# Grouped-query score maxima taken from high parts alone, in pairs on 64 rows each, eight pairs a chunk

## The chip, the cores and the metric

One core of one Trainium2 chip runs the whole kernel. The metric is the device time of one execution in microseconds. The engines are TensorE (PE in the profile; its weight loads are PEld), VectorE (DVE), ScalarE (ACT), GpSimd (POOL) and SyncE (SP, which issues most transfers). Each takes its own queue in order.

## The reference, cut to what matters

An encoder block on 2048 tokens of width 1024, in float32. Two groups of heads run side by side: multi-head latent attention (MLA, 8 heads of 96 dimensions) and grouped-query attention (GQA, 8 query heads of 64 dimensions on 2 key/value heads). Both are softmax attention over all 2048 keys:

```
s = jnp.einsum('bkgqd,bskd->bkgqs', qblk.astype(jnp.float32), kf) * scale
p = jax.nn.softmax(s, axis=-1)
return jnp.einsum('bkgqs,bskd->bkgqd', p, vf)
```

Norms and an axial rotation on queries and keys come before, an output projection, a residual add and a dense SwiGLU network behind.

## The kernel before

Operands of matmuls are split into a high part that fits the fast float32r format and a low part that holds the rest; a product is then high x high + high x low + low x high.

Four stages follow each other: the input projections (to about 440 us), attention (440 to 1885 us), the output projection, and the dense network. The change lies in attention, and a little in the end of the first stage.

Attention goes by chunks of 512 queries: 4 chunks a head, the 8 GQA heads first (chunks 0 to 31), then the 8 MLA heads (32 to 63). Within a chunk it goes by 16 key tiles of 128 keys; `g` counts key tiles over all chunks. For each key tile:

- `score` (L732, L733): two matmuls into a bank `sc`, keys on the stationary side. For GQA `kk` holds the high part of the keys on 64 rows and the low part on the other 64, `qh` holds the high queries twice, so one matmul of 128 rows gives high x high + low x high; the second adds high keys (`k1`) x low queries, and on a 65th row the shift, minus the query's maximum.
- `expo` and `high` (L742, L752, ACT): the exponential, and its high part `ph`. `low` (L756, DVE): its low part `pl`. In 4 of a GQA chunk's 16 tiles the low part is made by POOL, and a matmul with `tail1` (L795) adds up the rows.
- `pv_high`, `pv_low` (L786, L796): products with the values into the banks `px` and `py`.

At a chunk's end come `out_copy`, `out_x`, `out_y` (ACT L802, DVE L806, L810), `out_mm` (L819, L820: eight small matmuls on PE into an `mx` bank) and `out_div` (four small DVE operations, L827 to L830).

The shift needs the maxima ahead of the scores. `max_mm` (L702) computes a block of 128 queries x 512 keys roughly, for GQA with `qh` against `kk`; `max_reduce` (L707, DVE) takes its row maxima into `cm`. A chunk has 16 such blocks, numbered `m`; after the last, L709 (DVE) joins them, `shift_mm` (L713, PE) transposes them, and `shift_row` (L717, ACT) puts them, through a DMA, into the operand's extra row. Blocks run 24 ahead of the scores; the first 24 (`EARLY`) stand in the first stage.

PSUM has eight banks: 4 for `sc`, 2 for `mx`, 1 each for `px` and `py`. A tile of `mx` takes the two banks in turn and waits until the reader of the tile before the last is done. `mx` serves the maximum blocks, L713's output, `out_mm`, and for a few tiles of the first stage done late (`late_mm`, one set of four transposes in each of eight chunks) their transposes.

The order of PE, ACT, DVE and POOL is written out by a table: each operation gets a time in units of one key tile (`at`), operations are sorted by it, and every engine runs its own in that order. `GQA` and `MLA` hold the offsets: `S` for the score, `C` and `B` for high and low, `M` for the block of the maximum, `R` for its reduction, `Sh` and `Sc` for the shift. An `at` never goes ahead of the last one of the same function.

Of the kernel before, what the change touches and what calls it, by code (L numbers as in the profile page):

```python
# [20 lines left out]
P = 128  # L21
S = 2048
NT = S // P
D = 1024
KD = D // P
QL, KVL, ROPE, NOPE, QK, VD = 384, 256, 32, 64, 96, 64
H = 8
HD = 64
# [8 lines left out]
CH = 512  # L37
LK = H * QK
NCH = S // CH

# [6 lines left out]
def hybrid_block_kernel(  # L47
# [7 lines left out]
    nc = tc.nc  # L55
# [7 lines left out]

    d_qh = dram.tile([H, QK, S], F32, name="d_qh")
    d_ql = dram.tile([H, QK, S], F32, name="d_ql")
    d_kh = dram.tile([H, QK, S], F32, name="d_kh")
    d_kl = dram.tile([H, QK, S], F32, name="d_kl")
    d_gqh = dram.tile([H, HD, S], F32, name="d_gqh")
    d_gql = dram.tile([H, HD, S], F32, name="d_gql")
    d_gkh = dram.tile([GKV, HD, S], F32, name="d_gkh")  # L70
    d_gkl = dram.tile([GKV, HD, S], F32, name="d_gkl")
# [19 lines left out]
    def pst(tag=None):  # L91

        uid[0] += 1
        if "a" in pools:
            return pools["a"].tile([P, CH], F32, tag="pa", name=f"pa_{uid[0]}")
        if tag is None:
            tag = TURN[turn[0] % len(TURN)]
            turn[0] += 1
        return pools["b"].tile([P, CH], F32, tag=tag, name=f"{tag}_{uid[0]}", bufs=BANKS[tag])
# [4 lines left out]
    def fetch(dst, src):  # L104
        nc.sync.dma_start(dst.bitcast(F32), src)
# [439 lines left out]
    for t in range(3, LAST):  # L545
# [31 lines left out]
    EXB, PHB, PLB = 3, 5, 6  # L577
    AHEAD = 24
    EARLY = 24
    LATE = 29.4  # L580
    HEADAT = 12

    GQA = dict(
        S=-1.6, E=-0.05, C=0.6, B=1.2, Cq=0.85, Bp=1.9, A=1.4, M=1.7, R=0.65, Sh=1.6, Sc=1.9, px=5.45,
        py=7.45, X=0.6, Y=0.75, Z=0.7, T=3.6, D=1.49,
        dx=[0.0, -0.5, -0.5, -0.5, -0.3, 0.0, -0.3, -0.6, -0.6, -0.35, -0.35, -0.35, -0.35, 0.4, 0.4, -0.1],
        dy=[0.6, 0.55, 0.35, 0.35, 0.35, 0.35, 0.35, 0.35, 0.35, 0.35, 0.1, 0.1, 0.1, 0.1, 0.1, 0.1],
# [2 lines left out]
        S=-1.75, E=-0.05, C=0.7, B=1.4, Cq=0.8, Bp=1.4, A=1.35, M=-4.1, R=0.5, Sh=1.6, Sc=1.2, px=5.9,  # L592
# [11 lines left out]
    def load_head(n):  # L604
        h = ORDER[n]
        hd = heads[n] = {"mla": h < H, "col": h * VD}
        todo = []
        if h < H:
            hd["kh"] = kh = op.tile([QK + 1, S], F32R, tag="op0", name=f"kh_{h}")
            hd["kl"] = kl = op.tile([QK, S], F32R, tag="op1", name=f"kl_{h}")  # L610
            todo += [(kh[0:QK, :], d_kh[h]), (kl, d_kl[h])]
            one = kh[QK:QK + 1, :]
            vi = h
        else:
            g = h - H
            vi = H + g // (H // GKV)
            one = None
            if vi in shared:
                hd["kk"], hd["k1"], hd["v"] = shared[vi]
            else:  # L620
                hd["kk"] = kk = op.tile([P, S], F32R, tag="op0", name=f"kk_{h}")
                hd["k1"] = k1 = op.tile([HD + 1, S], F32R, tag="op1", name=f"k1_{h}")
                e = vi - H
                todo += [(kk[0:HD, :], d_gkh[e]), (kk[HD:P, :], d_gkl[e]), (k1[0:HD, :], d_gkh[e])]
                one = k1[HD:HD + 1, :]
        if n == 0:
            cut = S - 2 * P
            for dst, src in todo:
                fetch(dst[:, 0:cut], src[:, 0:cut])
            late.extend((dst[:, cut:S], src[:, cut:S]) for dst, src in todo)  # L630
        else:
            for dst, src in todo:
                fetch(dst, src)
        if one is not None:
            fetch(one, d_one)
            hd["v"] = v = op.tile([P, NT, VW], F32R, tag="opv", name=f"v_{h}")
            if n == 0:
                cut = LAST - 2
                fetch(v[:, 0:cut], d_v[vi][:, 0:cut])
                late.append((v[:, cut:], d_v[vi][:, cut:]))  # L640
            else:
                fetch(v, d_v[vi])
            if h >= H:
                shared[vi] = hd["kk"], hd["k1"], v
# [24 lines left out]
    cms, pms, pcs, scs, exs, phs, pls = {}, {}, {}, {}, {}, {}, {}  # L669
    accs, pxs, pys, o65s, pts = {}, {}, {}, {}, {}  # L670

    def mla(u):
        return heads_mla[u // NCH]
# [3 lines left out]
    def pace(u):  # L677
        return MLA if mla(u) else GQA
# [5 lines left out]
    def block(m):  # L684

        u, r = divmod(m, NT)
        return (u, r % 4, r // 4) if u == 0 else (u, r // 4, r % 4)

    def max_mm(m):
        u, qt, kc = block(m)  # L690
        hd = heads[u // NCH]
        if m % NT == 0:
            cms[u] = (bs.tile([P, 4, 4], F32, tag="cm", name=f"cm_{u}"),
                      bs.tile([P, 4], F32, tag="cx", name=f"cx_{u}"))
        qh = qs[u, 0]
        qt_ = slice(qt * P, (qt + 1) * P)
        ks = slice(kc * CH, (kc + 1) * CH)
        pms[m] = pm = pst("mx")
        if hd["mla"]:
            nc.tensor.matmul(pm, qh[0:QK, qt_], hd["kh"][0:QK, ks], start=True, stop=True)  # L700
        else:
            nc.tensor.matmul(pm, qh[:, qt_], hd["kk"][:, ks], start=True, stop=True)  # L702

    def max_reduce(m):
        u, qt, kc = block(m)
        cm, cx = cms[u]
        nc.vector.tensor_reduce(out=cm[:, qt, kc:kc + 1], in_=pms.pop(m), axis=AX.X, op=ALU.max)  # L707
        if m % NT == NT - 1:
            nc.vector.tensor_reduce(out=cx, in_=cm, axis=AX.X, op=ALU.max)  # L709
# [143 lines left out]
        transpose_split(d["mh"], d["ml"], o_sb[t // 4][:, t % 4, :], KD)  # L853

    def max_block(m):
        max_mm(m)
        max_reduce(m)


# [12 lines left out]
    def late_part(t, nm, b0, which):  # L872
        hi, lo = (room["qk".index(nm)][0:QK].rearrange("p (s h c) -> p s h c", s=2, c=P)[:, i] for i in range(2))
        t4_parts(banks[t, nm, b0], nm, b0, hi, lo, which)
        if b0 > 0 and which == "l":
            t4_store(t, nm, hi, lo)

    load_head(0)
    for u in range(QHB - 1):
        load_q(u, 0)  # L880
# [10 lines left out]
    for m in range(4):  # L891
        max_block(m)
# [7 lines left out]
    for m in range(4, 8):  # L900
        max_block(m)
# [4 lines left out]
    for m in range(8, 12):  # L906
        max_block(m)
# [28 lines left out]
    def at(key, fn, *args):  # L936
        key = max(key, latest.get(fn, key))
        latest[fn] = key
        ops.append((key, len(ops), fn, args))
        return key  # L940

    for g in range(TOTAL):
        u, kt = divmod(g, NT)
        i, q = g // 2, pace(u)
# [12 lines left out]
        if kt == NT - 1:  # L957
            at(kx + q["X"], out_copy, u)
            k = at(kx + q["Y"], out_x, u)
            k = at(max(k + 0.01, ky + q["Z"]), out_y, u)  # L960
            k = at(k + q["T"], out_mm, u)
            at(k + q["D"], out_div, u)
    for m in range(EARLY, TOTAL):
        u = m // NT
        q = pace(u)
        k = m - AHEAD + q["M"]
        at(k, max_mm, m)
        k = at(k + q["R"], max_reduce, m)
        if m % NT == NT - 1:
            k = at(k + q["Sh"], shift_mm, u)  # L970
            at(k + q["Sc"], shift_row, u)
    for n in range(1, len(ORDER)):
        at((n - 1) * NCH * NT + HEADAT if n > 1 else -99, load_head, n)
# [5 lines left out]
    for n, t in enumerate((LAST - 1, LAST)):  # L979
        k = LATE + 4 * n * NT  # L980
        at(k - 11, late_load, t)
# [275 lines left out]
    with tc.tile_pool(name="dg", reuse_waits="tile", bufs=6) as dg:  # L1257
# [19 lines left out]
        for T in range(2):  # L1277
# [4 lines left out]
            u = dg.tile([P, 4, CH], F32, tag="u", name=f"u_{T}", bufs=1)  # L1282
# [94 lines left out]
```

## Time and profile before

| | before |
|---|---|
| median of 3 runs | 3373.79 us (3369.88 to 3375.1) |
| profiled execution | 3374.82 us, span 3373.0 us |
| PE / DVE / ACT / POOL busy | 99% / 80% / 58% / 49% of the span |
| one GQA chunk (792.20 to 813.30) | 21.10 us: DVE busy 19.79, ACT 18.40, POOL 18.01 |
| granted TensorE clock | 0.997 of full speed |

A row of the timeline is: start in us from the span's start, how long it took, engine, line, operation, what it writes and reads, shapes, count, and in brackets the idle time of the engine ahead of it with what ended it. A row of the groups (section 5 of the page) ends with busy us, mean ns of one, and idle us ahead. A row of the waits is: who waited, for whom, us in total, how often, the longest. Ends of matmuls are modelled, so two starts tell more than a matmul's length.

### The profile page before, as it was taken

Reading aid. Unit: us, or ns where it says so; the run is one execution under the profiler, and the core shown is the slowest. Engines: PE = TensorE matmul, PEld = TensorE weight load, DVE = VectorE, ACT = ScalarE, POOL = GpSimd, SP = SyncE. Lnnn points to the kernel's source line nnn. Section 1 sums busy time; section 2 is a strip of 40 time slices with the busy share of each in tenths; the row PEclk is TensorE's granted clock in tenths of the full one; section 3 lists DMA queues with packets and bytes.
Section 4 is the critical chain, followed back from the end, with each engine's and each line's share of the span. In section 5 each row is a group of like instructions: output and inputs, shape, how many; then the busy total and the mean of one; then the engine's idle time right before and its main releaser. Section 6 shows DMA issues by size and latency. Waiting matters only on the chain.

```text
span 3373.0 us, 47535 instructions
## 1 busy us (share of the span) xinstructions
PE 3342.7 (99%) x15722; PEld 2693.6 (80%) x15722; DVE 2699.0 (80%) x4844; ACT 1967.5 (58%) x3726; POOL 1659.5 (49%) x1152
## 2 busy tenths in 40 slices
PE   8999999999999999999999999999999999999999
PEld 7999967777777777777777788878878888888887
DVE  6777799999999899999999656777787767776574
ACT  5444478888888778787878634332343333344443
POOL 4445478888887777777777301332312222130020
PEclk9999999999999999999999999999999999999999
DMA  5665621201000211111110456545464344486664
GB/s 175 148 146 135 152 75 48 60 20 51 20 20 14 70 48 50 51 46 32 34 51 19 129 179 235 181 146 159 156 198 143 125 146 145 146 273 229 219 199 164
DMA packets 330192, 390.96 MB, mean 116 GB/s; under 512 B 20719, under 2 KB 219980, under 8 KB 325264
## 3 DMA queue, kind: packets, MB, share of 16 engines
q1 hardware_dynamic: 329122, 387.72, 37.9%
q8 instruction: 124, 2.03, 0.2%
q14 instruction: 122, 1.00, 0.1%
q10 hardware_dynamic: 824, 0.21, 0.0%
HBM read 254.38 MB, written 133.34 MB: 115 GB/s over the span
## 4 chain that ended last, share of the span: by engine, by line
PE 84%; DVE 2%; issue 0%; ACT 0%; DMA 0%; DVEq 0%; SPq 0%; ACTq 0%
PE px L786 7%; PE py L796 7%; PE sc L154 7%; PE sc L153 7%; PE sc L152 7%; PE sc L732 4%; PE mx L700 4%; PE sc L733 4%; PE sc L730 4%; PE sc L728 4%; PE sc L729 3%; PE mx L154 3%; PE mx L152 3%; PE mx L153 3%; PE mx L702 3%; PE px L152 2%
## 5 line engine op out<-in xcount | busy, mean ns | idle before, releaser
L772 POOL TENSOR_TENSOR acc<-acc,ph 128x1024 f32<-128x1024 f32 x320 | 767.3, 2398 | 186.4 <-ACT ph L752 139.2
L707 DVE TENSOR_REDUCE cm<-mx 128x1 f32<-128x512 f32 x1000 | 680.8, 683 | 88.6 <-PE mx L700 44.0
L756 DVE TENSOR_TENSOR pl<-sc,ph 128x512 fp32r<-128x512 f32 x896 | 608.6, 679 | 10.7 <-ACT ph L752 10.6
L742 ACT ACTIVATE sc<-sc 128x512 f32<-128x512 f32 x896 | 525.4, 586 | 127.1 <-PE sc L730 52.2
L752 ACT CAST ph<-sc 128x512 fp32r<-128x512 f32 x896 | 525.2, 586 | 64.9 <-ACT cr L717 20.5
L796 PE MATMUL py<-pl,v 128*65 128x512 f32 x1024 | 399.4, 396 | 0.0
L786 PE MATMUL px<-ph,v 128*128 128x512 f32 x1024 | 394.5, 400 | 0.0
L1013 POOL TENSOR_TENSOR as_g<-rg 128x512 f32<-128x512 f32 x44 | 69.0, 1569 | 419.5 <-DMA rg<-in_w_gate_dram 280.7
L786 PEld LDWEIGHTS px<-ph,v 128*128 128x128 f32 x1024 | 193.8, 189 | 72.4 <-DVE xs L806 13.5
L1018 DVE TENSOR_TENSOR tl<-rt,th 128x512 fp32r<-128x512 f32 x154 | 120.9, 786 | 141.5 <-ACT th L1017 141.5
L1017 ACT CAST th<-rt 128x512 fp32r<-128x512 f32 x154 | 96.0, 623 | 224.7 <-PE py L153 98.2
L732 PE MATMUL sc<-qh,kk 128*128 128x512 f32 x512 | 206.5, 403 | 3.3 <-DMA d_v<-vst 1.8
L700 PE MATMUL mx<-kh,qh 96*128 96x512 f32 x512 | 206.3, 403 | 3.1 <-ACT cr L717 1.0
L728 PE MATMUL sc<-ql,kh 96*128 96x512 f32 x512 | 205.2, 401 | 0.6 <-DVE pl L756 0.6
L733 PE MATMUL sc<-ql,k 65*128 65x512 f32 x512 | 204.8, 400 | 0.0
L730 PE MATMUL sc<-qh,kh 97*128 97x512 f32 x512 | 203.0, 396 | 0.0
L729 PE MATMUL sc<-qh,kl 96*128 96x512 f32 x512 | 201.8, 394 | 0.0
L775 POOL TENSOR_TENSOR acc<-ph,ph 128x1024 f32<-128x1024 f32 x64 | 153.5, 2399 | 97.9 <-ACT ph L752 92.5
L702 PE MATMUL mx<-kk,qh 128*128 128x512 f32 x488 | 193.7, 397 | 0.0
L796 PEld LDWEIGHTS py<-pl,v 128*65 128x65 f32 x1024 | 140.6, 137 | 50.0
L763 POOL TENSOR_TENSOR pl<-ex,ph 128x1024 fp32r<-128x1024 f32 x64 | 151.8, 2394 | 0.6 <-PE sc L733 0.6
L1013 POOL TENSOR_TENSOR as_g<-rg,as_g 128x512 f32<-128x512 f32 x22 | 37.1, 1688 | 231.7 <-DVE al_g L1018 231.7
(593 smaller groups left out, 8972.1 us busy)
## 6 DMA issues: line engine op xcount, KB each, us to landing
rt<-d_a SPq DMA_DIRECT2D x154, 256.0 KB
rg<-in_w_gate_dram SPq DMA_DIRECT2D x44, 512.0 KB
ru<-in_w_up_dram SPq DMA_DIRECT2D x44, 512.0 KB
d_a<-ga SPq DMA_DIRECT2D x88, 256.0 KB
rw<-d_w SPq DMA_DIRECT2D x88, 256.0 KB
rw<-in_w_down_dram SPq DMA_DIRECT2D x66, 256.0 KB
x<-in_x_dram SPq DMA_DIRECT2D x32, 512.0 KB
wv<-in_w_down_dram SPq DMA_DIRECT2D x22, 512.0 KB
```

The source lines that it names most:

```text
L152: nc.tensor.matmul(dst, ah, bh, start=first, stop=False)
L700: nc.tensor.matmul(pm, qh[0:QK, qt_], hd["kh"][0:QK, ks], start=True, stop=True)
L707: nc.vector.tensor_reduce(out=cm[:, qt, kc:kc + 1], in_=pms.pop(m), axis=AX.X, op=ALU.max)
L728: nc.tensor.matmul(ps, hd["kh"][0:QK, ks], ql, start=True, stop=False)
L732: nc.tensor.matmul(ps, hd["kk"][:, ks], qh, start=True, stop=False)
L733: nc.tensor.matmul(ps, hd["k1"][:, ks], ql[0:HD + 1, :], start=False, stop=True)
L742: nc.scalar.activation(out=out, in_=scs.pop(g) if row_sum(i) else out, func=AF.Exp, scale=(QK if mla(g // NT) else HD) ** -0.5)
L752: nc.scalar.copy(part(phs, "ph", i, PHB)[:, e], scs[g])
L756: nc.vector.tensor_tensor(out=part(pls, "pl", i, PLB)[:, e], in0=scs.pop(g), in1=phs[i][:, e], op=ALU.subtract)
L772: nc.gpsimd.tensor_tensor(out=acc, in0=acc, in1=ph, op=ALU.add)
L786: nc.tensor.matmul(pxs[u], v[:, kt, 0:P], phs[g // 2][:, g % 2], start=kt == 0, stop=kt == NT - 1)
L796: nc.tensor.matmul(py, v[:, kt, VD:P + 1], pls[i][:, e], start=kt == 0, stop=kt == NT - 1)
```

## The change

For GQA the maximum is now taken from the high parts of queries and keys alone. That product has 64 rows, so two blocks, `m` and `m + 1`, stand next to each other on PE: the first on rows 0 to 63 (`k1` and the first copy of `qh`), the second on rows 64 to 127 (`kk`, whose halves are swapped so that the high keys lie there, and the second copy of `qh`). Each writes its own `mx` bank. The matmul of a pair is issued at the even block; the reductions stay one for each block. In the table of times the blocks of a GQA chunk are put 0.75 of a key tile apart (`G`) instead of 1, so the eight pairs fill 12 of the 16 key tiles; `M`, `Sh`, `Sc` and `LATE` change with it.

```
-    LATE = 29.4
+    LATE = 25.1
...
-        S=-1.6, E=-0.05, C=0.6, B=1.2, Cq=0.85, Bp=1.9, A=1.4, M=1.7, R=0.65, Sh=1.6, Sc=1.9, px=5.45,
+        S=-1.6, E=-0.05, C=0.6, B=1.2, Cq=0.85, Bp=1.9, A=1.4, M=4.9, G=0.75, R=0.65, Sh=1.3, Sc=1.6, px=5.45,
...
-                todo += [(kk[0:HD, :], d_gkh[e]), (kk[HD:P, :], d_gkl[e]), (k1[0:HD, :], d_gkh[e])]
+                todo += [(kk[0:HD, :], d_gkl[e]), (kk[HD:P, :], d_gkh[e]), (k1[0:HD, :], d_gkh[e])]
...
     def max_mm(m):
...
-        pms[m] = pm = pst("mx")
         if hd["mla"]:
-            nc.tensor.matmul(pm, qh[0:QK, qt_], hd["kh"][0:QK, ks], start=True, stop=True)
-        else:
-            nc.tensor.matmul(pm, qh[:, qt_], hd["kk"][:, ks], start=True, stop=True)
+            pms[m] = pm = pst("mx")
+            nc.tensor.matmul(pm, qh[0:QK, qt * P:(qt + 1) * P], hd["kh"][0:QK, kc * CH:(kc + 1) * CH],
+                             start=True, stop=True)
+            return
+        for e, (rows, kb) in enumerate(((slice(0, HD), hd["k1"]), (slice(HD, P), hd["kk"]))):
+            _, qt, kc = block(m + e)
+            pms[m + e] = pm = pst("mx")
+            nc.tensor.matmul(pm, qh[rows, qt * P:(qt + 1) * P], kb[rows, kc * CH:(kc + 1) * CH],
+                             start=True, stop=True)
...
     def max_block(m):
-        max_mm(m)
+        if mla(m // NT) or m % 2 == 0:
+            max_mm(m)
         max_reduce(m)
...
-        k = m - AHEAD + q["M"]
-        at(k, max_mm, m)
+        k = (u * NT + q["G"] * (m % NT) if "G" in q else m) - AHEAD + q["M"]
+        if mla(u) or m % 2 == 0:
+            k = at(k, max_mm, m)
         k = at(k + q["R"], max_reduce, m)
```

Line numbers after are some lines higher: the maximum matmul L702 becomes L706, its reduction L707 becomes L712, the subtraction L756 becomes L761, L806 becomes L811, L810 becomes L815, L713 becomes L718, and scores and products (L732, L733, L786, L795, L796) L737, L738, L791, L800, L801.

On PE, at the end of a chunk's maxima, the order before, with the waits of each row (`mx_996` and so on are the blocks, `qh_15` the chunk whose maxima are taken, `sc` scores of chunk 14):

```order
L702 MATMUL mx_996_9457<-kk_8_5348,qh_15_9139 128x512 [waits DVE_49]
L786 MATMUL px_991_9431<-ph_113_9391,v_8_5354 128x512
L796 MATMUL py_997_9464<-pl_112_9369,v_8_5354 65x512 [waits DVE_49]
L732 MATMUL sc_998_9467<-qh_14_8897,kk_8_5348 128x512
L733 MATMUL sc_998_9467<-ql_14_9137,k1_8_5349 128x512
L702 MATMUL mx_999_9470<-kk_8_5348,qh_15_9139 128x512 [waits DVE_49]
L796 MATMUL py_997_9464<-pl_112_9369,v_8_5354 65x512
L786 MATMUL px_991_9431<-ph_114_9418,v_8_5354 128x512
L732 MATMUL sc_1000_9479<-qh_14_8897,kk_8_5348 128x512
L733 MATMUL sc_1000_9479<-ql_14_9137,k1_8_5349 128x512
L702 MATMUL mx_1001_9484<-kk_12_9051,qh_16_9373 128x512 [waits DMAHW3_49,DMAHW1_49,DVE_49]
```

One block stands in each key tile, and the next chunk's first block follows the last of this one. The same place after, from the last pair on:

```order
L706 MATMUL mx_996_9457<-k1_8_5349,qh_15_9133 128x512 [waits DVE_49]
L706 MATMUL mx_997_9459<-kk_8_5348,qh_15_9133 128x512 [waits DVE_49]
L791 MATMUL px_991_9430<-ph_113_9387,v_8_5354 128x512
L801 MATMUL py_998_9466<-pl_112_9363,v_8_5354 65x512
L737 MATMUL sc_999_9469<-qh_14_8891,kk_8_5348 128x512
L738 MATMUL sc_999_9469<-ql_14_9131,k1_8_5349 128x512
L801 MATMUL py_998_9466<-pl_112_9363,v_8_5354 65x512
L791 MATMUL px_991_9430<-ph_114_9419,v_8_5354 128x512
L737 MATMUL sc_1000_9479<-qh_14_8891,kk_8_5348 128x512
L738 MATMUL sc_1000_9479<-ql_14_9131,k1_8_5349 128x512
L801 MATMUL py_998_9466<-pl_113_9396,v_8_5354 65x512
L718 MATMUL mx_1001_9486<-ident_76,cx_15_9301 4x128 [waits DVE_49]
```

The pair's two matmuls stand next to each other, each with a wait for the bank of its own, and behind them come scores and products with no block among them; the next pair is 13 matmuls of 512 columns and the eight small ones of `out_mm` further down.

On DVE, at the end of a chunk's reductions, before (`cm_15` is the chunk's maxima):

```order
L707 TENSOR_REDUCE cm_15_9248<-mx_987_9405 128x1 [waits PE_49]
L806 TENSOR_TENSOR xs1_6029<-px_955_9197,xs1_6029 64x512 [waits Activation_49]
L756 TENSOR_TENSOR pl_114_9425<-sc_984_9387,ph_114_9418 128x512 [waits Pool_49]
L707 TENSOR_REDUCE cm_15_9248<-mx_989_9420 128x1 [waits PE_49]
L756 TENSOR_TENSOR pl_114_9425<-sc_986_9400,ph_114_9418 128x512 [waits Activation_49]
L707 TENSOR_REDUCE cm_15_9248<-mx_992_9435 128x1 [waits PE_49]
```

And the corresponding place after, in a later chunk of the same order:

```order
L712 TENSOR_REDUCE cm_19_10236<-mx_1128_10327 128x1 [waits PE_49]
L761 TENSOR_TENSOR pl_145_10332<-sc_1124_10307,ph_145_10323 128x512 [waits Activation_49]
L712 TENSOR_REDUCE cm_19_10236<-mx_1129_10329 128x1 [waits PE_49]
L712 TENSOR_REDUCE cm_19_10236<-mx_1132_10350 128x1 [waits PE_49]
L811 TENSOR_TENSOR xs1_6029<-px_1099_10132,xs1_6029 64x512 [waits Activation_49]
L761 TENSOR_TENSOR pl_146_10361<-sc_1127_10319,ph_146_10355 128x512 [waits Pool_49]
L712 TENSOR_REDUCE cm_19_10236<-mx_1133_10352 128x1 [waits PE_49]
```

Four reductions stand to two subtractions, where three stood; a chunk's reductions are denser in one part and absent from the rest.

More of the change, by code (lines that the diff above doesn't have):

```diff
@@ L695, in max_mm @@
         qh = qs[u, 0]
-        qt_ = slice(qt * P, (qt + 1) * P)
-        ks = slice(kc * CH, (kc + 1) * CH)
-        pms[m] = pm = pst("mx")
         if hd["mla"]:
-            nc.tensor.matmul(pm, qh[0:QK, qt_], hd["kh"][0:QK, ks], start=True, stop=True)
-        else:
-            nc.tensor.matmul(pm, qh[:, qt_], hd["kk"][:, ks], start=True, stop=True)
+            pms[m] = pm = pst("mx")
[7 more added lines that the diff above has]
+                             start=True, stop=True)
     def max_reduce(m):
```

## The prediction

> **What bounds the kernel now.** I read the page first: busy shares, then the costliest groups.
>
> ```profile
> span 3373.0 us, 47535 instructions
> PE 3342.7 (99%) x15722; PEld 2693.6 (80%) x15722; DVE 2699.0 (80%) x4844; ACT 1967.5 (58%) x3726; POOL 1659.5 (49%) x1152
> ...
> L707 DVE TENSOR_REDUCE cm<-mx 128x1 f32<-128x512 f32 x1000 | 680.8, 683 | 88.6 <-PE mx L700 44.0
> L756 DVE TENSOR_TENSOR pl<-sc,ph 128x512 fp32r<-128x512 f32 x896 | 608.6, 679 | 10.7 <-ACT ph L752 10.6
> ```
>
> The 99% of PE says little by itself, since the ends of matmuls are modelled. What the change touches is the stage of the grouped heads (GQA), so I looked at single chunks there. One chunk runs from one L713 (the transpose that ends a chunk's maxima) to the next; then the same chunk in the windows view, with an early chunk (537.30) that also carries late work of stage A; then the waits in 665 to 1066 us.
>
> ```profile
> 792.18 0.27 PE L713 MATMUL mx<-ident,cx 128*4 128x128 f32 x1
> ...
> 813.26 0.27 PE L713 MATMUL mx<-ident,cx 128*4 128x128 f32 x1
> ```
>
> ```profile
> core 0: us, PE busy (x) PEld busy (x) DVE busy (x) ACT busy (x) POOL busy (x), PEclk, DMA share, GB/s
> 792.20:813.30 21.10, 21.10 (x101) 15.83 (x100) 19.79 (x36) 18.40 (x33) 18.01 (x9) 1.00 0.06 20
> ...
> 537.30:558.80 21.50, 21.50 (x104) 16.19 (x104) 20.23 (x37) 18.57 (x34) 17.94 (x9) 1.00 0.30 92
> ```
>
> ```profile
> DVE cm L707 <- PE mx L702: 15.5, 57, 0.4
> ...
> PEld px L786 <- DVE xs L806: 8.1, 19, 0.4
> ```
>
> A chunk takes 21.1 us (21.5 early). In the second window, 19 chunks long, the reductions wait for the maximum matmuls 57 times, and no maximum matmul waits for a reduction. So PE sets the pace, with DVE close behind: 19.8 of 21.1 us. Its price per matmul, and that of the transposes at a chunk's end:
>
> ```profile
> 812.15 0.22 PE L819 MATMUL mx<-ident,o 65*128 65x65 f32 x1
> ...
> 813.37 0.19 PEld L732 LDWEIGHTS sc<-qh,kk 128*128 128x128 f32 x1
> ...
> 813.60 0.39 PE L732 MATMUL sc<-qh,kk 128*128 128x512 f32 x1
> ...
> 816.41 0.39 PE L702 MATMUL mx<-kk,qh 128*128 128x512 f32 x1
> ```
>
> From 813.60 to 816.41 stand 13 matmuls, 12 steps: 0.234 us each. A weight load starts when the matmul before its own begins to stream, so 812.15 to 813.37 is the whole of L819, L820 and L713: 1.22 us. A chunk has 84 matmuls of 512 columns (16 maxima, 32 scores, 32 on V, 4 tails): 84 x 0.234 + 1.22 = 20.9, and 21.1 with a wait at L786.
>
> DVE, from the same chunk:
>
> ```profile
> 793.43 0.69 DVE L707 TENSOR_REDUCE cm<-mx 128x1 f32<-128x512 f32 x1
> ...
> 796.43 0.68 DVE L756 TENSOR_TENSOR pl<-sc,ph 128x512 fp32r<-128x512 f32 x1
> ...
> 803.99 0.68 DVE L707 TENSOR_REDUCE cm<-mx 128x1 f32<-128x512 f32 x1
> 804.76 0.68 DVE L806 TENSOR_TENSOR xs<-px,xs 64x512 f32<-64x512 f32 x1
> 805.37 0.67 DVE L756 TENSOR_TENSOR pl<-sc,ph 128x512 fp32r<-128x512 f32 x1
> ```
>
> Five steps in 3.00 us: a reduction or a subtraction takes 0.60 of DVE, however long its row; L806 adds 0.17 ahead of itself.
>
> And the two hand-overs between the engines:
>
> ```profile
> 451.68 0.68 DVE L707 TENSOR_REDUCE cm<-mx 128x1 f32<-128x512 f32 x1
> ...
> 452.42 0.19 PEld L702 LDWEIGHTS mx<-kk,qh 128*128 128x128 f32 x1 [0.21 <-DVE cm L707]
> ...
> 452.52 0.14 PEld L796 LDWEIGHTS py<-pl,v 128*65 128x65 f32 x1
> ```
>
> ```profile
> 801.15 0.39 PE L702 MATMUL mx<-kk,qh 128*128 128x512 f32 x1
> ...
> 801.59 0.69 DVE L707 TENSOR_REDUCE cm<-mx 128x1 f32<-128x512 f32 x1 [0.35 <-PE mx L702]
> ```
>
> The wait sits on the weight load. From the end of a reduction (452.36) to the load is 0.05, and 0.11 later the next load shows that the matmul streams: 0.16 in all. From a matmul's start to its reduction: 0.44.
>
> **The change, part by part.** *The arithmetic of a pair.* Sixteen matmuls become eight pairs on two halves of the rows. Before shows no such pair. Bounds: the second costs nothing (8 x 0.234 = 1.9 us less PE in a chunk) or a full 0.234 (no gain). I take "nothing", but for the sum it hardly matters, as shown below. The rows that DVE reduces are the same in number and shape; the order of the halves of kk and the missing low part cost no instruction.
>
> *The order.* This is what decides. Call the blocks of pair p A(p) and B(p). There are two mx banks, so B(p) needs the bank of B(p-1): PE, which takes its queue in order, stands at B(p) until DVE has reduced B(p-1), and all behind it (scores, V) stands too. With G = 0.75 the eight pairs are packed into 12 of a chunk's 16 key tiles; the rest has no maxima. Counted in the order (the text on the change shows two places of it), between B(p) and A(p+1) stand 7, 7, 8, 5, 7, 5, 7 matmuls, and between B(8) and the next chunk's A(1) 22, with L819, L820 and L713 among them. Before, one block stood in each key tile. On DVE, from the reduction of A(1) to that of B(7), 25 operations follow each other: 14 reductions, 9 subtractions (L756), L806 and L810; in the sparse rest are B(8) and A(8), 3 subtractions and the small ones.
>
> The period of a chunk cannot be less than the way round this ring:
> - DVE, start of A(1)'s reduction to the end of B(7)'s: 24 steps x 0.60 + 0.17 + 0.69 = 15.3.
> - Hand-over to B(8): 0.16.
> - PE, B(8) and 22 matmuls: 23 x 0.234 = 5.4, and 1.22: 6.6.
> - A(1) of the next chunk to its reduction: 0.44.
>
> Sum 22.5, against 21.1 now. The legs do not overlap: in the first PE waits at the pairs (its own work there, 46 x 0.234 + 8 x 0.234 = 12.6, is less than 15.3), in the second DVE waits for PE (its work there is some 3 us).
>
> Inside the first leg DVE has waits of its own. A(p+1) can be reduced no sooner than 0.16 + (n+1) x 0.234 + 0.44 after the reduction of B(p-1), with n matmuls between the pairs: 2.5 for n = 7, 2.7 for 8. DVE comes there after 4 operations, 2.3 to 2.4. Walking through the pairs it waits about 0.1 at the 2nd and 3rd, 0.3 at the 4th, 0.15 at the 6th; at 5 and 7 (n = 5) nothing. That is 0.6, so 23.1. If the two matmuls of a pair do not overlap at all, B(1) and its followers come 0.23 later, most of which lies under B's wait: 0.2 more a chunk.
>
> ACT and POOL (18.4 and 18.0 of 21.1 busy) have room in 23.1. The score of a key tile stands 2.8 tiles ahead of its subtraction, 3.9 us at the slower pace, which covers two ACT operations. M, Sh and Sc move the shift row (with its DMA on ACT's queue) into the sparse part, where PE passes 22 matmuls before A(1) needs it: covered. The late transposes (LATE) also move there and cost PE what they cost before, 0.4 in eight chunks.
>
> *The sum.* 29 rounds from the third chunk of the stage to the last: 29 x 2.0 = 58. The last chunk's dense part ends with no round behind it: A(1) to B(8) takes 16.4 us, where 10.5 tiles took 10.5 x 21.1 / 16 = 13.8: 2.6 more. In stage A 12 blocks, now pairs, are done early:
>
> ```profile
> 401.20 1.17 PE L702 MATMUL pa<-kk,qh 128*128 128x512 f32 x4
> ...
> 431.74 0.49 PE L702 MATMUL pa<-kk,qh 128*128 128x512 f32 x1 [0.57 <-DVE cm L707]
> ```
>
> Four in a row there take 4 x 0.26; 24 blocks halved would give 2.9, nothing if the waits for DVE stay; I take 1 less. The multi-head latent (MLA) part keeps order and shapes. 58 + 2.6 - 1 = 60. The profiled execution took 3374.8 (span 3373.0), 1.0 above the median 3373.8: 3433 against the median.
>
> *A rule weighed.* L713 has four columns, a tile shape other than its neighbours':
>
> ```profile
> 451.44 0.39 PE L796 MATMUL py<-pl,v 128*65 128x512 f32 x1
> ...
> 451.67 0.27 PE L713 MATMUL mx<-ident,cx 128*4 128x128 f32 x1
> ...
> 451.78 0.19 PEld L732 LDWEIGHTS sc<-qh,kk 128*128 128x128 f32 x1
> ```
>
> It follows L796 after the usual 0.23, though that runs to 451.83 by its row, and the matmul behind it streams 0.11 later, one weight load. So a change of shape by columns does not wait for the array to empty; one by rows is not shown. The Trainium skill, "TensorEngine Tiling (Array Packing)", Key Properties, says that a change of the tiling mode, unlike a change of tile, drains TensorE; by that rule the time would be that of the second rival below. The trace speaks against it for columns and is silent on rows.
>
> The Trainium skill, "TensorE: Matmul & The Clock Gate", Part 3, says matmuls on different row groups run at once, about 4 ns apart. By it a pair costs one matmul, 3433; with no overlap the ring gives 29 x 0.2 = 6 more, 3439. No run here shows a pair yet.
>
> **The rivals.**
> 1. *The pairs' gain comes through, faster.* PE has 1.9 us less to do in a chunk, until DVE is full: 21.1 - 19.8 = 1.3 x 30 = 39: 3335. For it: PE is the bound now. Against it: it needs the banks of a pair free whenever PE comes, that is DVE's part per pair (25 operations for 7 pairs, 2.1 us) below PE's (54 x 0.234 / 8 = 1.6). It decides from there: only where DVE's step were 0.44 instead of 0.60. Chance 0.07.
> 2. *The rows' switch empties the array.* Each way then costs the rest of the matmul before (0.39 - 0.23 = 0.16) and a bare weight load (0.11): 0.53 a pair. In the ring that comes on the waits at pairs 2, 4, 6 and behind B(8): 4 x 0.53 = 2.1 a chunk, 29 x 2.1 = 61: 3494. For it: nothing in the trace; L713 against. Chance 0.09.
> 3. *No change that can be measured.* The ring would have to be 2 us shorter, as if the sparse part held 13 matmuls instead of 22. Chance 0.04.
>
> **How the numbers follow.** The forecast has 0.78: 3433, of its own between 3412 (the bare ring, 29 x 1.4 = 41, and no end) and 3452 (no overlap, and 0.4 a chunk of waits for ACT or POOL that I did not see). 0.02 stays for slower cases I have not named. The range goes beyond the forecast's ends by what the hand-overs leave unsure, and a part of a drain: 3406 to 3470; outside it lie rivals 1 to 3 nearly whole, so it leaves out 0.2. Faster by over 0.2% (6.7 us, about what a measurement of this kernel can tell from no change) 0.07, same 0.04, slower 0.89 (0.78 + 0.09 + 0.02).
>
> **What would show it.** In the profile after: L713's successor every 23.1 us in the GQA stage (23.5 early); waits of the weight load of a pair's second matmul for a reduction, some 3 to 4 us a chunk, where there were none; DVE down to 86% of a chunk, with its idle time in one place, ahead of A(1)'s reduction; 22 matmuls there at 0.234. A pair's two starts a few ns apart where both banks were free. MLA chunks unchanged. I am wrong if DVE's row stays near 94% and PE shows no waits at the pairs, or if reductions step faster than 0.60.

## The result, and the profile after

| | before | after |
|---|---|---|
| median | 3373.51 us (4 runs) | 3502.99 us (4 runs, 3499.29 to 3504.34) |
| ratio | | 1.0384, 95% interval 1.0366 to 1.0402 |
| span of the profiled execution | 3373.0 us | 3500.6 us |
| one GQA chunk, steady / with late work of the first stage | 21.1 / 21.5 us | 25.0 / 26.3 us |

The change is slower, as forecast, but by 129 us instead of 60. It lies outside the range, a little beyond the second rival's 3494, but the two parts that make it up have other sizes than that rival's (see below).

The page after, its busy shares and the two groups that were shown of before:

```profile
span 3500.6 us, 47531 instructions
PE 3442.2 (98%) x15722; PEld 2658.1 (76%) x15722; DVE 2708.8 (77%) x4844; ACT 1976.2 (56%) x3726; POOL 1656.5 (47%) x1152
...
L712 DVE TENSOR_REDUCE cm<-mx 128x1 f32<-128x512 f32 x1000 | 679.4, 683 | 120.3 <-PE mx L706 64.1
L761 DVE TENSOR_TENSOR pl<-sc,ph 128x512 fp32r<-128x512 f32 x896 | 608.7, 680 | 75.2 <-ACT ph L757 73.4
```

The work is the same: as many matmuls and DVE operations, of the same length. The loss is time in which PE streams no columns (waits, and weight loads with no matmul beside them), and PE's 98% hides it. The single chunk shows it, from one L718 to the next, and its window:

```profile
866.40 0.27 PE L718 MATMUL mx<-ident,cx 128*4 128x128 f32 x1
...
891.42 0.27 PE L718 MATMUL mx<-ident,cx 128*4 128x128 f32 x1
```

```profile
core 0: us, PE busy (x) PEld busy (x) DVE busy (x) ACT busy (x) POOL busy (x), PEclk, DMA share, GB/s
866.40:891.42 25.02, 24.06 (x98) 14.59 (x97) 19.92 (x35) 18.55 (x33) 17.94 (x9) 1.00 0.05 17
```

25.0 us at full clock; DVE is busy for 19.9 of them, as in the 21.1 before, so 80% instead of the 86% that the forecast had. The waits in 665 to 1066 us, which is 16 chunks:

```profile
DVE cm L712 <- PE mx L706: 35.5, 63, 0.8
PEld mx L706 <- DVE cm L712: 35.1, 77, 0.6
PEld mx L706 <- issue: 30.9, 83, 0.4
```

The second line is the forecast's new wait, PE at a pair for the bank that a reduction must free: 2.2 us a chunk, where there was none. The third is not in the forecast: a maximum block's weight load starts late though nothing that the profile can name holds it, 0.37 us each time. One undisturbed pair, PE's rows and then its weight loads:

```profile
870.50 0.39 PE L791 MATMUL px<-ph,v 128*128 128x512 f32 x1
870.81 0.50 PE L706 MATMUL mx<-k,qh 64*128 64x512 f32 x1
870.82 0.49 PE L706 MATMUL mx<-kk,qh 64*128 64x512 f32 x1
871.24 0.50 PE L737 MATMUL sc<-qh,kk 128*128 128x512 f32 x1
```

```profile
870.81 0.18 PEld L706 LDWEIGHTS mx<-k,qh 64*128 64x128 f32 x1 [0.35 <-issue]
...
871.24 0.19 PEld L737 LDWEIGHTS sc<-qh,kk 128*128 128x128 f32 x1 [0.24 <-issue]
871.35 0.19 PEld L738 LDWEIGHTS sc<-ql,k 65*128 65x128 f32 x1
```

Elsewhere a weight load runs under the matmul before it. Here the pair's first load starts 0.31 after L791, when that would have streamed for 0.23: 0.08 of waiting, then 0.11 of a load with nothing beside it. The same comes again at L737. L738's load shows that L737 streams from 871.35, so from the end of L791's step (870.50 + 0.23) the pair took 0.62 us. Two matmuls on all rows take 0.47. The two of this pair do start 0.01 apart, and the second is nearly free; but going from 128 rows to 64 and back costs 0.19 each way, which is more than it saves.

Most pairs do not get even that. In this chunk the two matmuls start within 0.02 of each other in only three of the eight pairs. In the others the second comes 0.14 to 0.74 later; in three of these its load waits for a reduction to free its bank, in two the profile names no wait. The last pair:

```profile
888.05 0.49 PE L706 MATMUL mx<-k,qh 64*128 64x512 f32 x1
888.79 0.49 PE L706 MATMUL mx<-kk,qh 64*128 64x512 f32 x1 [0.25 <-DVE cm L712]
889.21 0.50 PE L791 MATMUL px<-ph,v 128*128 128x512 f32 x1
```

In 665 to 1066 us it is 38 of 128 pairs that start within 0.03.

The 127.6 us by which the span grew, by stretches, cut at the chunks' L718: 4.1 up to the first of attention, 41.9 in the next 9 chunks, 79.8 in the 20 steady ones (4.0 each), 5.3 in the 3 around the switch to MLA, and -3.5 in all the rest.

### The profile page after: what moved, and what is told of

Same layout as the page of the kernel before. It is cut to its first block, busy times and chain, and to the rows that moved or that the text cites. A ratio compares the mean times of both kernels' runs of the same rounds, so it can differ in the third digit from the quotient of the medians.

```text
span 3500.6 us, 47531 instructions
## 1 busy us (share of the span) xinstructions
PE 3442.2 (98%) x15722; PEld 2658.1 (76%) x15722; DVE 2708.8 (77%) x4844; ACT 1976.2 (56%) x3726; POOL 1656.5 (47%) x1152
## 4 chain that ended last, share of the span: by engine, by line
PE 79%; DVE 6%; ACT 1%; issue 1%; POOL 0%; DMA 0%; ACTq 0%; DVEq 0%; POOLq 0%
PE sc L154 7%; PE sc L153 7%; PE sc L152 7%; PE px L791 7%; PE py L801 6%; PE mx L700 3%; PE mx L706 3%; PE mx L154 3%; PE mx L152 3%; PE mx L153 3%; PE sc L733 3%; PE sc L735 3%; PE sc L734 3%; DVE cm L712 3%; PE sc L737 3%; PE sc L738 3%
## 5 line engine op out<-in xcount | busy, mean ns | idle before, releaser
L712 DVE TENSOR_REDUCE cm<-mx 128x1 f32<-128x512 f32 x1000 | 679.4, 683 | 120.3 <-PE mx L706 64.1
L761 DVE TENSOR_TENSOR pl<-sc,ph 128x512 fp32r<-128x512 f32 x896 | 608.7, 680 | 75.2 <-ACT ph L757 73.4
L791 PE MATMUL px<-ph,v 128*128 128x512 f32 x1024 | 406.1, 412 | 12.2 <-DVE xs L811 12.2
L801 PE MATMUL py<-pl,v 128*65 128x512 f32 x1024 | 403.0, 399 | 0.0
L791 PEld LDWEIGHTS px<-ph,v 128*128 128x128 f32 x1024 | 194.9, 190 | 105.9 <-DVE xs L811 25.7
L737 PE MATMUL sc<-qh,kk 128*128 128x512 f32 x512 | 215.1, 420 | 2.8 <-DVE cm L712 1.5
L738 PE MATMUL sc<-ql,k 65*128 65x512 f32 x512 | 206.1, 402 | 0.2 <-DMA ql<-cr 0.2
L733 PE MATMUL sc<-ql,kh 96*128 96x512 f32 x512 | 205.2, 401 | 0.6 <-DVE pl L761 0.6
L801 PEld LDWEIGHTS py<-pl,v 128*65 128x65 f32 x1024 | 141.2, 138 | 58.8 <-issue 14.7
L1024 ACT CAST ah_g<-as_g 128x512 fp32r<-128x512 f32 x88 | 54.7, 621 | 157.1 <-PE sc L153 74.6
```

The source lines that it names most:

```text
L737: nc.tensor.matmul(ps, hd["kk"][:, ks], qh, start=True, stop=False)
L761: nc.vector.tensor_tensor(out=part(pls, "pl", i, PLB)[:, e], in0=scs.pop(g), in1=phs[i][:, e], op=ALU.subtract)
L791: nc.tensor.matmul(pxs[u], v[:, kt, 0:P], phs[g // 2][:, g % 2], start=kt == 0, stop=kt == NT - 1)
L801: nc.tensor.matmul(py, v[:, kt, VD:P + 1], pls[i][:, e], start=kt == 0, stop=kt == NT - 1)
```

## The experiments

The theory after the result: two costs of about equal size add up, the ring of the forecast (PE waits at the second of a pair for DVE) and the change of the rows' shape. The rival: the shape costs little by itself, and the ring is dearer than forecast, because the 64-row blocks' reductions come late or because ACT and POOL are late. Nine kernels ran, each timed against before on the same chip. In the table "twos" are two matmuls on all 128 rows, one right behind the other; "singles" stand alone; "packed" is the changed table of times.

| kernel | blocks | table of times | ratio (95%) | median us | steady chunk us |
|---|---|---|---|---|---|
| after | pairs, 64 rows | packed | 1.0384 (1.0366 to 1.0402) | 3503.0 | 25.0 |
| e1 | twos, 128 rows | packed | 1.0238 (1.0223 to 1.0253) | 3453.5 | 23.5 |
| e5 | twos, 128 rows | as before | 1.0188 (1.0173 to 1.0203) | 3438.3 | 23.0 |
| e8 | singles, 128 rows | packed | 1.0119 (1.0104 to 1.0134) | 3415.9 | 22.3 |
| e2 | pairs, 64 rows | as before | 1.0334 (1.0316 to 1.0351) | 3485.9 | 24.3 |
| e7 | half of the pairs on 64 rows | packed | 1.0314 (1.0297 to 1.0331) | 3479.6 | 24.3 |
| e4 | e1, short reductions | packed | 1.0102 (1.0087 to 1.0117) | 3409.1 | 22.1 |
| e6 | after, short reductions | packed | 1.0229 (1.0213 to 1.0244) | 3452.1 | 23.5 |
| e3 | singles, 64 rows | as before | 1.0718 (1.0663 to 1.0772) | 3622.1 | 26.5 |
| e9 | as before, one product later | one number | 0.9999 (0.9990 to 1.0008) | 3372.5 | 21.1 |

**e1: after's order without the change of shape.** Both matmuls of a pair use all 128 rows.

```
-            nc.tensor.matmul(pm, qh[rows, qt * P:(qt + 1) * P], kb[rows, kc * CH:(kc + 1) * CH],
+            nc.tensor.matmul(pm, qh[:, qt * P:(qt + 1) * P], hd["kk"][:, kc * CH:(kc + 1) * CH],
```

> The changed kernel with its order kept (G = 0.75, M, Sh, Sc, LATE), but each pair made of two matmuls on all 128 rows, as before the change: no change of tile shape on TensorE. Packing (the ring of two banks, my forecast): a GQA chunk takes 23.1 to 23.6 us, 3436 to 3450 us in all. Switch (only the change to 64 rows costs, the order is harmless): 21.1 us a chunk, about 3374. Both: the part of the 129 us that this run keeps is the order's, the rest the switch's.

3453.5: some 3 us above the upper end. So 80 of the 129 us are the order's and 49 the shape's. Of these 49, 5 are there by the first L718 of attention (455.8 after, 450.6 here), where the granted clock differs too (last section). The ring can be read in this kernel's trace, in one steady chunk (rows of PE, of DVE and of the weight loads):

```profile
843.15 0.61 PE L706 MATMUL mx<-kk,qh 128*128 128x512 f32 x2
...
866.65 0.62 PE L706 MATMUL mx<-kk,qh 128*128 128x512 f32 x2
```

```profile
843.58 0.69 DVE L712 TENSOR_REDUCE cm<-mx 128x1 f32<-128x512 f32 x1 [0.57 <-PE mx L706]
...
858.57 0.69 DVE L815 TENSOR_TENSOR o<-py,xs 65x512 f32<-65x512 f32 x1 [0.33 <-PE py L801]
859.18 1.96 DVE L712 TENSOR_REDUCE cm<-mx 128x1 f32<-128x512 f32 x3
...
867.08 0.69 DVE L712 TENSOR_REDUCE cm<-mx 128x1 f32<-128x512 f32 x1 [0.60 <-PE mx L706]
```

```profile
859.91 0.19 PEld L706 LDWEIGHTS mx<-kk,qh 128*128 128x128 f32 x1 [0.89 <-DVE cm L712]
```

From A(1)'s reduction (843.58) to B(8)'s load 16.33 us, from there to the next A(1) 6.74, and 0.43 to its reduction: 23.5. The forecast had 15.9 + 0.05, 0.11 + 6.6, and 0.44. Its one miss is in the first leg, mostly the 0.33 in which L815 waits for PE, which is late itself.

**e5 and e8: which half of the order costs.** e5 is e1 with the table of before (`M=1.7, Sh=1.6, Sc=1.9, LATE=29.4`, no `G`): two blocks at once, but not packed. e8 is before with the packed table (`M=4.9, G=0.75, Sh=1.3, Sc=1.6, LATE=25.1`): packed, but one block at a time.

> The table of before (blocks spread over all 16 key tiles), but two matmuls on all 128 rows issued together at every even block, as in e1: neither packed nor on 64 rows. If it is enough for a stall that a two needs both banks at once: the waits of e2 (24.3 us a chunk, of which TensorE's own work is 22.0) remain without the switches, 21.1 + 1.5 = 22.6 us a chunk, about 3420. If packing alone costs: 3374.

> The kernel before with single blocks on 128 rows, each in its own place, but packed by the changed table (0.75 of a key tile apart, 12 of 16 tiles). Packing (the ring through VectorE's 25 operations and TensorE's 22 matmuls does not need pairs): 22.5 to 23.1 us a chunk, with the dearer early chunks 3418 to 3440. Pairing (the stall comes from two matmuls in a row alone): 21.1 us, 3374.

e5 gave 3438, 65 above before and 18 above what was expected; e8 gave 3416, 42 above before and just under its expected 3418 to 3440. Either alone costs, and they do not add (together 80). e5's waits in the same stretch:

```profile
DVE cm L712 <- PE mx L706: 39.2, 69, 1.2
PEld mx L706 <- DVE cm L712: 32.8, 52, 0.9
```

Both engines wait for each other in turn. The waits fit this reading: two banks taken at once leave no block ahead, so DVE has nothing to reduce while PE waits for a bank, and PE has no bank while DVE reduces. Before, the first line had 15.5 us and the second did not exist.

**e2, e7: how much the shape costs.** e2 is after with the table of before. e7 is after with only every second pair on 64 rows:

```
+        halves = (slice(0, HD), hd["k1"]), (slice(HD, P), hd["kk"])
+        for e, (rows, kb) in enumerate(halves if m % 4 == 0 else ((slice(0, P), hd["kk"]),) * 2):
```

> Pairs on 64 rows as in the changed kernel, but the table of before (one block a key tile, M = 1.7, Sh = 1.6, Sc = 1.9, LATE = 29.4). Packing: with the blocks spread the pairs' gain comes through until VectorE is full, 19.8 us a chunk, about 3335. Switch: a pair costs 0.62 us instead of 2 x 0.233, so TensorE has 68 x 0.233 + 8 x 0.62 + 1.2 + 0.2 = 22.2 us a chunk, about 3408, more if a pair waits for a bank that the chunk's end holds.

> The changed kernel with every second pair on 128 rows, the others on 64: half of the switches. If the switch accounts for what lies between e1 (3454) and the changed kernel (3503): half way, 3478. If instead something else in the 64-row form does (the operands, the early blocks): not half way.

e2 missed by far: 3486, since I had left out that two at once costs with the blocks spread as well (e5's 65). Against e5, the kernel of the same order, it is 47.6 longer: the shape's price again. e7 came out as expected (3478): 3479.6, which is 26.0 above e1 and 23.4 below after. Half the changes of shape, half the cost.

**e4, e6: DVE's leg taken down.** In both, GQA's maxima are taken over only the first half of a block's columns, so that a reduction is shorter (0.42 us by its row, 0.33 to the next operation); e4 is e1 with it, e6 after with it.

```
-        nc.vector.tensor_reduce(out=cm[:, qt, kc:kc + 1], in_=pms.pop(m), axis=AX.X, op=ALU.max)
+        nc.vector.tensor_reduce(out=cm[:, qt, kc:kc + 1], in_=pms.pop(m)[:, 0:CH if mla(u) else CH // 2], axis=AX.X, op=ALU.max)
```

> As e1 (packed order, 128 rows), and the GQA reductions take the maximum over the first half of each block's columns alone, so VectorE's step for them falls from 0.60 to about 0.33 us. Packing: VectorE's leg of the ring loses 14 x 0.27 = 3.8 us, the ring falls below TensorE's own 21.1, and the time is back at about 3374. If the packed order costs by something other than VectorE's reductions, the time stays near that of e1.

> The changed kernel with GQA reductions over the first half of each block's columns alone, as in e4, whose pairs were on 128 rows. There VectorE no longer binds, so the difference to e4 is the switch on TensorE by itself. Switch (a pair 0.62 us, two full matmuls 0.47): 8 x 0.155 = 1.2 us a chunk more than e4's 22.05, 23.3 us, 3447. Without a price of the switch: pairs save 1.9 us a chunk, 20.2 us or what else binds, below 3400.

e4 gave 3409: 44 of the order's 80 us went with DVE's time, not all. So DVE is in the ring, as forecast, but the order keeps 35 us of its own. In e4's waits the bank is still one of them, at a fifth of e1's 59.4:

```profile
DVE cm L712 <- PE mx L706: 58.0, 91, 1.0
...
PEld mx L706 <- DVE cm L712: 11.9, 36, 0.4
```

What the rest is made of can be separated only in part. One part stands at B(8), in a chunk of e4 (rows of DVE, then the load):

```profile
787.19 0.69 DVE L815 TENSOR_TENSOR o<-py,xs 65x512 f32<-65x512 f32 x1 [0.59 <-PE py L801]
787.79 0.75 DVE L712 TENSOR_REDUCE cm<-mx 128x1 f32<-128x256 f32 x2
```

```profile
788.32 0.19 PEld L706 LDWEIGHTS mx<-kk,qh 128*128 128x128 f32 x1 [0.68 <-PE mx L706]
```

B(7)'s reduction, the first of the two, stands in DVE's queue behind L815, which has waited for PE; it ends at 788.21, and B(8)'s load comes 0.11 later. B(8) follows A(8) by 0.67 instead of 0.23, so this is 0.44 of the 1.0 us by which the chunk is longer than before's. It is a wait that shorter reductions do not remove.

e6 came near what was expected (3447), 3452, 43.0 above e4: with DVE out of the way the change of shape costs nearly what it did, so the ring does not hide it.

**e3: one block at a time on 64 rows.** Before, with GQA's maximum matmul on the first 64 rows alone:

```
-            nc.tensor.matmul(pm, qh[:, qt_], hd["kk"][:, ks], start=True, stop=True)
+            nc.tensor.matmul(pm, qh[0:HD, qt_], hd["kk"][0:HD, ks], start=True, stop=True)
```

> The kernel before with its order, one block a key tile, but the matmul of a GQA block takes the high parts alone, 64 rows, with no partner. Packing: nothing changes, 3374. Switch: each of the 16 blocks of a chunk pays the way in and the way out, 0.38 us: 6.1 us a chunk, 30.5 chunks, 186 us, and 24 early blocks another 9: about 3565.

A steady chunk takes 26.5 instead of 21.1, 5.4 more where 6.1 were expected, for sixteen changes of shape instead of eight. One of them (PE's row, then the loads):

```profile
900.52 0.39 PE L796 MATMUL py<-pl,v 128*65 128x512 f32 x1
```

```profile
900.84 0.18 PEld L702 LDWEIGHTS mx<-kk,qh 64*128 64x128 f32 x1 [0.42 <-issue]
901.26 0.19 PEld L786 LDWEIGHTS px<-ph,v 128*128 128x128 f32 x1 [0.24 <-issue]
901.37 0.19 PEld L732 LDWEIGHTS sc<-qh,kk 128*128 128x128 f32 x1
```

By the same count as above, 901.37 - 900.52 - 0.23 = 0.62: a single block costs what a pair costs. The median is 57 us more than expected, by something else: in the profiled execution (3589, the shortest of four) the first three chunks of attention took 34 to 47 us each, at about half the clock (last section), and the longer executions have a still lower mean clock (0.968 at 3630 us, against 0.981).

**e9: the wait that before has at L786.** `dx[0]` of GQA from 0.0 to 0.47, so that the product stands behind the reader it waits for.

> The kernel before, and only the first product px of each GQA chunk moved half a key tile later (dx of tile 0 from 0.0 to 0.47), behind one low product and one maximum, to cover the stall of TensorE at L786 that the profile of before shows once a chunk (0.42 us idle of the weight load, some 0.27 of a matmul's step). If that stall is TensorE's own loss: 20.8 us a chunk instead of 21.07, 30 x 0.27 = 8 us less, 3365. If VectorE or GpSimd hold the chunk instead: no change, 3374.

No change: 0.9999. The wait at L786 only moved to a score's weight load, where it stands for ACT (in 665 to 1066 us that row has 9.5 us, 4.6 in before):

```profile
PEld sc L732 <- ACT ex L742: 9.5, 19, 0.5
```

No kernel here is faster than before.

## Why the prediction was wrong

**What failed: "The arithmetic of a pair".** It priced a pair between one matmul (0.234) and two (0.468), and took the change of shape at nothing because L713, with four columns, showed none. That analogy was the error: L713 has few columns but all 128 rows. The change of rows costs 0.19 us each way, so a pair takes 0.62, outside both bounds. It measured 49 (after against e1), 48 (e2 against e5) and 43 us (e6 against e4), and half of it with half the changes (e7). Eight times the 0.15 between 0.62 and 0.47 is 1.2 a chunk, and the steady chunks show 1.3 (e2), 1.4 (e6) and 1.5 (after); the difference fits the pairs whose second matmul comes late, but was not tried apart. The order alone, e1's 3453.5, lies inside the range; the shape's price brings the time out of it. I had the mechanism as the second rival, at 0.27 each way and 61 us, and gave it 0.09. That 0.27 took the modelled length of the matmul before (0.39) as the time to empty the array; the rows show 0.08, not 0.16. That its 3494 comes so near 3503 is partly luck: it adds 61 for the shape, which cost 49, to 60 for the order, which cost 80. The right bound for something that the trace did not show was zero to the rival's full price, and the chance nearer one half.

The Trainium skill, "TensorEngine Tiling (Array Packing)", Key Properties, says that a change of the tiling mode drains TensorE. The runs agree for rows, with 0.19 us each way, in so far as the next load starts only 0.08 after the step of the matmul before; that this is the drain and not another hold on the load was not tried. The Trainium skill, "TensorE: Matmul & The Clock Gate", Part 3, says that different row groups run at once. The runs agree where both banks are free: the two starts lie 0.01 us apart, and a single block (0.62) costs as much as such a pair.

**"The order": near in size, loose in cause.** The forecast's ring, without the shape, is e1: 23.5 a chunk against 23.1, and 80 against 60 us. The wait it named is there, at B's weight load, 3.5 us a chunk in e1 (59.4 us in 17 chunks) against 3 to 4, and the reductions step by 0.60:

```profile
PEld mx L706 <- DVE cm L712: 59.4, 120, 0.9
```

DVE does wait mostly in the sparse part ahead of A(1), but not in one place, and more for ACT than for A(1): in the chunk above 1.32 and 0.41 at two subtractions, for their `ph`, and 0.60 at A(1)'s reduction. In after it also waits at three reductions behind A(1)'s (0.34, 0.61 and 0.45 in the chunk shown). The longest of these waits in e1's chunk:

```profile
862.66 0.69 DVE L761 TENSOR_TENSOR pl<-sc,ph 128x512 fp32r<-128x512 f32 x1 [1.32 <-ACT ph L757]
```

And I laid the ring to the packing, while e5 shows 65 us without any. Taking both banks at once costs more by itself than packing (42), and since the two do not add, the 80 cannot be divided between them. The forecast's own lower and upper ends, added up again from their terms, come out 1 to 2 us off (3413 or 3414 for 3412, 3450 or 3451 for 3452), which changes nothing.

**"23.5 early": mis-sized.** The chunks with late work took 25.0 in e1 and 26.3 after. In e1's rows of such a chunk B(1) waits for L835, the last reader of `out_mm`'s bank, which comes later behind a set of transposes that also takes a turn of the `mx` banks. B(1) follows A(1) by 0.62 instead of 0.23, so that is 0.4 of the 1.5 us; the rest I did not divide, and nothing of it was tried.

```profile
628.57 0.40 PE L706 MATMUL mx<-kk,qh 128*128 128x512 f32 x1
629.19 0.47 PE L706 MATMUL mx<-kk,qh 128*128 128x512 f32 x1 [0.22 <-DVE o L835]
```

**"I take 'nothing'" for the second matmul: true of few pairs.** The two overlap where both banks are free, which is three of eight in the chunk shown. What the 0.2 a chunk for no overlap amounts to was not measured apart. That the arithmetic of a pair "hardly matters" failed by the shape: what lies between a B that waits and its followers is not covered, since after the wait comes the way back to 128 rows (B at 888.79, L791's row 0.42 later).

**The other steps** held: no more instructions, and MLA and what follows change by -3.5 us in all, of which little can be told from nothing: behind the last L713 before and e9, alike there, differ by 2.6. The first rival (faster) fell because a pair takes PE 0.62 instead of 0.47, so that there was no gain to come through, and because PE waits for DVE's banks.

**"1 less" in stage A:** at that stage's own L718 (row at 427.8 after, 428.0 before) it is 0.2, too little to tell from nothing: before and e9, alike up to there, differ by 1.1 (428.0 and 426.9). The 4.1 lost by the next L718 (455.8 against 451.7; 450.6 in e1) come where the granted clock is low (last section). In stage A several of the pairs stand two in a row:

```profile
408.57 0.49 PE L706 MATMUL pa<-k,qh 64*128 64x512 f32 x1
408.58 0.49 PE L706 MATMUL pa<-kk,qh 64*128 64x512 f32 x1
408.91 0.39 PE L706 MATMUL pa<-k,qh 64*128 64x512 f32 x1
408.91 0.39 PE L706 MATMUL pa<-kk,qh 64*128 64x512 f32 x1
```

The second pair follows without a new change, 0.34 later of which 0.11 is the first pair's bare load. So by an estimate from these rows four blocks between matmuls of 128 rows would take 0.86 (0.62 + 0.23) instead of 4 x 0.23 = 0.93. That is the smallest group at which halving the rows would pay here, and in attention it would need four `mx` banks where there are two. No run tried it.

## What to carry to other kernels

Matmuls on half the rows, two at a time, save streaming but pay for going to that shape and back (here 0.39 us together against 0.23 saved): group several pairs (by the estimate above), or leave the rows full. Two tiles that must both be free before PE goes on took away the slack of a double buffer here, and the engines' busy shares did not show it: count what each side does while the other holds both. An operation that the trace does not show is not bounded by one that differs from its neighbours in another way; give the unpriced mechanism its full cost as a bound, and a chance to match.

## What the runs showed of the hardware that I had not expected

A change of the number of rows between matmuls cost 0.19 us each way (0.08 of idle time and 0.11 of a weight load that no longer runs under a matmul). A change of columns (L713, which follows the matmul before it after the usual 0.23), or from 128 rows to 65 (L738 behind L737 in the prediction's 0.23 steps), showed none of this wait.

The granted clock at the start of attention was lowest in the kernels that have all of their blocks on 64 rows. The windows 440 to 460 us of before and of after:

```profile
440.00:460.00 20.00, 19.53 (x77) 14.09 (x76) 18.12 (x30) 18.58 (x35) 16.23 (x7) 0.90 0.14 39
```

```profile
440.00:460.00 20.00, 19.73 (x50) 11.42 (x48) 11.17 (x18) 14.60 (x27) 11.88 (x5) 0.57 0.07 19
```

0.90 against 0.57, and 50 matmuls done instead of 77. With full rows it was 0.86 in e1 and 0.89 in e5, with half the pairs still 0.86 (e7), and with all of them 0.77 (e6) and 0.71 (e2); each figure is of one execution. In e3, with single 64-row blocks, it stayed near half speed for over 100 us:

```profile
480.00:580.00 100.00, 100.00 (x231) 53.25 (x229) 48.59 (x82) 44.80 (x76) 38.04 (x18) 0.56 0.06 16
```

After 580 us it was 1.00. In after it was back at 1.00 in the window from 460 us, so the most that it can have cost there is some 9 us of the 129 (20 x 0.43), of which before lost 2 itself (20 x 0.10). That 64-row blocks are the cause, and not the slower start itself, was not tried apart.
